# A row-wise log-sum-exp: late sums held in PSUM, an earlier word to SyncE, and a first load cut in three

## The chip, the cores and the metric

The kernel runs on one core of a Trainium2 chip. Its time is device time in microseconds (us), from launch to completion on that core. Three runs of the kernel before the change took 162.76, 163.02 and 163.10 us; the median is 163.02 us.

A core has five engines that matter here, each with an instruction queue of its own: TensorE (PE in the profile), VectorE (DVE), ScalarE (ACT), GpSimd (POOL) and SyncE (SP). They meet only through semaphores. Here SyncE issues every DMA transfer. A transfer is spread over 16 DMA engines, and its semaphore counts 16 when all of them are done.

## The reference

The input is 32 x 512 x 1024 float32 values, 67.1 MB. For each of the 16384 rows of 1024 values the result is one number:

```python
x_max = np.max(x, axis=axis, keepdims=True)
return (x_max.squeeze(axis) + np.log(np.sum(np.exp(x - x_max), axis=axis))).astype(np.float32)
```

Every input byte has to be read from memory once, an exponential has to be taken of every element, and 1024 of them have to be added for each row. The output is only 64 KB.

## The kernel before, in words

**Layout.** The 16384 rows are dealt over 128 partitions, 128 rows to a partition, so that partition p holds rows 128p to 128p+127. What the kernel calls a row (or a slot of its ring) is one such row in every partition: 128 x 1024 floats, 0.524 MB. 

**No maximum in the fast path.** The kernel takes `exp(x)` without subtracting the maximum, adds, and takes the logarithm. At the end it judges whether that was safe: all row sums must lie between `LOW` and `HIGH` (1e-18 and 1e18). Only if some sum does not, a branch (`nc.If`, line 278) does the whole work again with the maximum subtracted. With the input given here the branch's body is skipped.

**The stream.** The 128 rows are cut into 17 loads (`CHUNKS`, line 10) of 4, 15, 16, 16, 16, 14, 13, 9, 7, 5, 4, 3, 2 and four times 1 rows. Loads go into a ring of 51 rows (`ring`, line 74). `load(i)` (line 125) makes SyncE wait until the ring slots are free again and then issues the transfer; each load has its own semaphore `landed[i]`. ScalarE waits for it, takes exp in place (line 196, in one or two parts), and VectorE adds up the rows (line 216; some loads row by row with a fused add, line 203). A few rows are summed by ScalarE itself, through the accumulator that an activation can carry along (`accum_out`, lines 223 and 186). The loads are small at the end, so that little work is left when the last bytes land.

**What comes ahead of everything.** The instructions of the first load are moved by hand (lines 323 to 331) to the front of the program's head, ahead of the drain with which SyncE enters the barrier that all engines pass at the start. So the first transfer is issued at the very start of the profiled span, and the second only after the barrier.

**The late rows.** The last four rows (`LATE`) are loaded one by one and summed by ScalarE into four columns of `late`. In the kernel before, `late` is a part of an SBUF tensor `checked`, which has the columns LOW, late sums, HIGH side by side. 

**The end.** ScalarE takes the logarithm of the four late sums (line 152, called from line 234), and SyncE stores the result (line 237). Beside that runs the judgement: VectorE finds the largest and the smallest of the 124 earlier sums (lines 242 and 245) and puts them next to the late ones; when ScalarE has delivered the last sum, one comparison (line 252) tests `LOW < value` and `value < HIGH` together; TensorE adds the 128 x 12 answers over the partitions (line 257); VectorE adds them up to one number, `verdict` (line 262). SyncE, VectorE and ScalarE wait for it, load it into a register (line 267) and branch on it (line 278). Behind the branch VectorE and ScalarE each add one to the semaphore `passed` (lines 314 and 315). SyncE waits for two of these, clears the semaphores, waits for the store and is done (lines 316 to 319).

The diff touches one long function; it is printed here with the line numbers that the profile uses.

Of the kernel before, what the change touches and what calls it, by code (L numbers as in the profile page):

```python
# [17 lines left out]
RING_ROWS = 51  # L18


UNEVEN = ()
PARTS = ((0, 128, 2), (1, 128, 4), (3, 128, 8), (7, 64, 8), (71, 128, 8))


LN_AT = 7
# [6 lines left out]
LOW, HIGH = 1e-18, 1e18  # L32


STEPS = (43, 43, 42)
# [3 lines left out]
def kernel(  # L39
# [6 lines left out]
    nc = tc.nc  # L46
# [22 lines left out]
    spans = list(zip((0, *CUTS), (*CUTS, D)))  # L69
    assert 1 <= len(spans) <= 2  # L70
    n_late = LATE - 1 + len(spans)
    K = n_late + 2

    ring = nc.alloc_sbuf_tensor("ring", [P, RING_ROWS, D], fp32).ap()
    sums = nc.alloc_sbuf_tensor("sums", [P, NB], fp32).ap()
    res = nc.alloc_sbuf_tensor("res", [P, NB], fp32).ap()

    checked = nc.alloc_sbuf_tensor("checked", [P, 3 * K], fp32).ap()
    good = nc.alloc_sbuf_tensor("good", [P, 2 * K], bf16).ap()
    ones = nc.alloc_sbuf_tensor("ones", [P, 1], bf16).ap()  # L80
    verdict = nc.alloc_sbuf_tensor("verdict", [1, 1], int32).ap()
    peak = nc.alloc_sbuf_tensor("peak", [P, NB], fp32).ap()
    votes = nc.alloc_psum_tensor("votes", [P, 512], fp32).ap()
    late = checked[:, K : 2 * K]
    ALL_GOOD = P * 2 * K

    landed = [nc.alloc_semaphore(f"landed{i}") for i in range(len(CHUNKS) + len(spans) - 1)]
    act_done = nc.alloc_semaphore("act_done")
# [36 lines left out]
    def load(i):  # L125
        (s, row), r = place[i], CHUNKS[i][0]
        act_wait = max(a for a, _ in busy[s : s + r])
        dve_wait = max(d for _, d in busy[s : s + r])
        if dve_wait:
            nc.sync.wait_ge(dve_done, dve_wait)  # L130
        if act_wait:
            nc.sync.wait_ge(act_done, act_wait)
        dst, src = ring[:, s : s + r], x_v[:, row : row + r]
        if i == len(CHUNKS) - 1:
            for k, (lo, hi) in enumerate(spans):
                nc.sync.dma_start(out=dst[:, :, lo:hi], in_=src[:, :, lo:hi]).then_inc(
                    landed[i + k], 16
                )
        elif i in UNEVEN:
            for first, last, step in PARTS:  # L140
                nc.sync.dma_start(
                    out=dst[first:last:step], in_=src[first:last:step]
                ).then_inc(landed[i], 16)
        else:
            nc.sync.dma_start(out=dst, in_=src).then_inc(landed[i], 16)
# [20 lines left out]
    n_early = len(body.instructions)  # L166

    nc.scalar.preload_act_table_set("natural_log_exp_and_others")  # L168
    nc.gpsimd.memset(checked[:, :K], LOW)  # L169
    nc.gpsimd.memset(checked[:, 2 * K :], HIGH)  # L170
    nc.gpsimd.memset(ones, 1.0).then_inc(pool_done, 1)  # L171

    logged = 0
    done_before = [(0, 0)]
    for i, (r, n_dve, parts, by_halves) in enumerate(CHUNKS):
        if i:
            load(i)
        s, row = place[i]
        if i == LN_AT:
            logged = place[i - LN_LAG][1]  # L180
            take_logs(0, logged, sums[:, :logged], *done_before[i - LN_LAG])
        if i == len(CHUNKS) - 1:
            take_logs(logged, late_row, sums[:, logged:late_row], *done_before[-LATE])
            for k, (lo, hi) in enumerate(spans):
                nc.scalar.wait_ge(landed[i + k], 16)
                nc.scalar.activation(  # L186
                    out=ring[:, s, lo:hi],
                    in_=ring[:, s, lo:hi],
                    func=Exp,
                    accum_out=late[:, LATE - 1 + k : LATE + k],  # L190
                ).then_inc(act_done, 1)
                acts += 1
            continue
        nc.scalar.wait_ge(landed[i], 16 * (len(PARTS) if i in UNEVEN else 1))
        for lo, hi in cuts(n_dve, parts):
            nc.scalar.activation(  # L196
                out=ring[:, s + lo : s + hi], in_=ring[:, s + lo : s + hi], func=Exp
            ).then_inc(act_done, 1)
            acts += 1
            nc.vector.wait_ge(act_done, acts)  # L200
            if by_halves:
                for j in range(lo, hi):
                    nc.vector.tensor_tensor_reduce(  # L203
                        out=ring[:, s + j, : D // 2],
                        in0=ring[:, s + j, : D // 2],
                        in1=ring[:, s + j, D // 2 :],
                        scale=1.0,
                        scalar=0.0,
                        op0=Alu.add,
                        op1=Alu.add,  # L210
                        accum_out=sums[:, row + j : row + j + 1],
                    ).then_inc(dve_done, 1)
                    dves += 1
                    busy[s + j] = (0, dves)
            else:
                nc.vector.reduce_sum(  # L216
                    out=sums[:, row + lo : row + hi], in_=ring[:, s + lo : s + hi], axis=AX
                ).then_inc(dve_done, 1)
                dves += 1
                for j in range(lo, hi):  # L220
                    busy[s + j] = (0, dves)
        for j in range(n_dve, r):
            nc.scalar.activation(  # L223
                out=ring[:, s + j],
                in_=ring[:, s + j],
                func=Exp,
                accum_out=total(row + j),
            ).then_inc(act_done, 1)
            acts += 1
            busy[s + j] = (acts, 0)  # L230
        done_before.append((dves, acts))

    summed = acts
    take_logs(late_row, NB, late[:, : NB - late_row], dves, acts)

    nc.sync.wait_ge(act_done, acts)
    nc.sync.dma_start(out=out_v, in_=res).then_inc(stored, 16)


    nc.vector.wait_ge(act_done, done_before[-LATE][1])  # L240
    nc.vector.wait_ge(dve_done, dves)
    nc.vector.reduce_max(  # L242
        out=late[:, n_late : n_late + 1], in_=sums[:, :late_row], axis=AX
    ).then_inc(dve_done, 1)
    nc.vector.tensor_reduce(  # L245
        out=late[:, n_late + 1 : n_late + 2], in_=sums[:, :late_row], axis=AX, op=Alu.min
    ).then_inc(dve_done, 1)
    dves += 2
    nc.vector.wait_ge(pool_done, 1)
    nc.vector.wait_ge(dve_done, dves)  # L250
    nc.vector.wait_ge(act_done, summed)  # L251
    nc.vector.tensor_tensor(  # L252
        out=good, in0=checked[:, : 2 * K], in1=checked[:, K:], op=Alu.is_lt
    ).then_inc(dve_done, 1)
    dves += 1
    nc.tensor.wait_ge(dve_done, dves)
    nc.tensor.matmul(  # L257
        votes[:1, : 2 * K], lhsT=ones, rhs=good, start=True, stop=True
    ).then_inc(counted, 1)
    nc.vector.wait_ge(counted, 1)  # L260
    with nc.allow_low_precision(reason="whole numbers"):
        nc.vector.reduce_sum(out=verdict, in_=votes[:1, : 2 * K], axis=AX).then_inc(judged, 1)  # L262
# [7 lines left out]
    ends = [sum(STEPS[: k + 1]) for k in range(len(STEPS))]  # L270
    steps = [(end - n, end) for n, end in zip(STEPS, ends)]
    base_dve, base_act = dves, acts
    PIECES = 3

# [39 lines left out]
    nc.vector.sem_inc(passed, 1)  # L314
    nc.scalar.sem_inc(passed, 1)
    nc.sync.wait_ge(passed, 2)
    nc.sync.sem_clear(range(used[0], used[-1] + 1))
    nc.sync.wait_ge(stored, 16)
# [48 lines left out]
```

## Time and profile before

| | value |
|---|---|
| median of 3 runs | 163.02 us |
| the profiled execution, its own time | 163.09 us |
| its span, first to last instruction | 161.7 us |
| read from memory, mean rate over the span | 67.11 MB, 415 GB/s |
| time of the DMA packets, share of 16 engines' span | 96.9% |
| DVE busy | 121.8 us (75%), 50 instructions |
| ACT busy | 115.2 us (71%), 40 instructions |
| PE, POOL busy | 0.2 us, 0.4 us |

How to read it. The span is 1.4 us shorter than the execution's own time; what lies around it is the program's start and end. A group of instructions is given by its source line, engine and operation, with output <- input, shapes, count, then busy time and mean duration, and last the time that its engine sat idle ahead of it and what ended that wait. The chain that ended last is followed back from the last instruction: each piece is either work or a transfer that somebody waited for. Instructions that only wait, set a register, branch or add to a semaphore are not in the busy times, but waits on them are listed (as DVEq, SPq and so on, the engine's queue). The table of stretches gives, for each stretch of the span, its length, the busy time and the number of instructions of PE, its weight loads, DVE, ACT and POOL, then the granted clock of TensorE, the DMA share and the rate in GB/s. A packet is put down to the stretch where it began, so that short stretches can show shares over 1.

Behind these views the trace keeps a record of each DMA packet (begin, duration, size), of each semaphore step and of each instruction, waits and branches too. Where a number in this document comes from such a record, it says so.

### The profile page before, as it was taken

The page shows a single profiled execution, that of the slowest core. Times are in us where ns is not written, and L with a number is a line of the kernel's source. Part 1 is how long each engine was busy: PE and PEld are TensorE (multiplying, and loading weights), DVE is VectorE, ACT ScalarE, POOL GpSimd, SP SyncE. Part 2 cuts the span into 40 slices and gives each one's busy share as a digit, 9 for nine tenths or more (in the row PEclk, how much of TensorE's full clock was granted, in tenths as well). Part 3 has the DMA queues.
Part 4 walks back from the last instruction along what each step waited for, and adds up shares of the span by engine and source line. Part 5 has one row for each costly group of instructions (what it writes and reads, how often), then busy time and mean ns, then how long its engine had stood idle before and what let it go on. Part 6 is the DMA issues. An engine that isn't in the chain of part 4 may idle for free.

```text
span 161.7 us, 145 instructions
## 1 busy us (share of the span) xinstructions
PE 0.2 (0%) x1; PEld 0.1 (0%) x1; DVE 121.8 (75%) x50; ACT 115.2 (71%) x40; POOL 0.4 (0%) x7
## 2 busy tenths in 40 slices
PE   0000000000000000000000000000000000000000
PEld 0000000000000000000000000000000000000000
DVE  0028000004999999999999599999999999999793
ACT  3170006995089960999429993999199999999995
POOL 0000000000000000000000000000000000000000
DMA  7999699979979979979979999999999999999990
GB/s 259 503 486 471 274 471 519 470 308 519 470 308 519 470 308 519 470 308 519 470 318 411 454 454 438 421 421 421 457 429 429 404 440 416 412 442 406 412 373 16
DMA packets 2592, 67.18 MB, mean 415 GB/s; under 512 B 288, under 2 KB 416, under 8 KB 928
## 3 DMA queue, kind: packets, MB, share of 16 engines
q1 hardware_dynamic: 2592, 67.18, 96.9%
HBM read 67.11 MB, written 0.07 MB: 415 GB/s over the span
## 4 chain that ended last, share of the span: by engine, by line
DMA 49%; DVE 30%; ACT 20%; issue 0%; PE 0%; DVEq 0%
DMA ring<-in_x_dram 49%; DVE sums L216 29%; ACT ring L196 17%; ACT ring L223 2%; ACT ring L186 1%; ACT res L152 0%; PE votes L257 0%; DVE good L252 0%; DVE verdict L262 0%; DVEq L251 0%
## 5 line engine op out<-in xcount | busy, mean ns | idle before, releaser
L216 DVE TENSOR_REDUCE sums<-ring 128x8 f32<-128x8192 f32 (+5 forms) x14 | 111.2, 7994 | 37.1 <-ACT ring L196 37.1
L196 ACT ACTIVATE ring<-ring 128x8192 f32<-128x8192 f32 (+6 forms) x18 | 104.4, 5836 | 43.8 <-DMA ring<-in_x_dram 43.6
L203 DVE CUSTOM_DVE_ANT_0 ring<-ring 128x512 f32<-128x512 f32 x16 | 9.9, 688 | 0.0
L223 ACT ACTIVATE ring<-ring 128x1024 f32<-128x1024 f32 x8 | 8.3, 1041 | 0.0
L168 ACT ACT_TABLE_LOAD x1 | 1.3, 1283 | 0.8 <-PEq L348 0.8
L223 ACT ACTIVATION_READ_ACCUMULATOR ring<-ring 128x1 f32 x8 | 1.5, 187 | 0.0
L203 DVE DVE_READ_ACCUMULATOR2_ANT sums<- 128x1 f32 x16 | 1.3, 84 | 0.0
L186 ACT ACTIVATE ring<-ring 128x1024 f32<-128x1024 f32 x1 | 1.0, 1039 | 0.0
L252 DVE TENSOR_TENSOR good<-checked 128x12 bf16<-128x12 f32 x1 | 0.2, 170 | 1.0 <-ACT ring L186 1.0
L152 ACT ACTIVATE res<-sums 128x81 f32<-128x81 f32 (+1 forms) x2 | 0.5, 240 | 0.0
L242 DVE TENSOR_REDUCE checked<-sums 128x1 f32<-128x124 f32 x1 | 0.3, 282 | 0.1
L262 DVE TENSOR_REDUCE verdict<-votes 1x1 int32<-1x12 f32 x1 | 0.2, 158 | 0.3 <-PE votes L257 0.3
L257 PE MATMUL votes<-good,ones 128*1 128x12 bf16 x1 | 0.2, 172 | 159.9 <-DVE good L252 159.9
L245 DVE TENSOR_REDUCE checked<-sums 128x1 f32<-128x124 f32 x1 | 0.3, 271 | 0.0
L152 ACT ACTIVATE res<-checked 128x4 f32<-128x4 f32 x1 | 0.2, 205 | 0.0
L186 ACT ACTIVATION_READ_ACCUMULATOR ring<-ring 128x1 f32 x1 | 0.2, 186 | 0.0
L257 PEld LDWEIGHTS votes<-good,ones 128*1 128x1 bf16 x1 | 0.1, 79 | 159.9 <-DVE good L252 159.9
L169 POOL MEMSET checked<- 128x6 f32 x1 | 0.1, 105 | 0.3 <-POOLq L348 0.3
L170 POOL MEMSET checked<- 128x6 f32 x1 | 0.1, 104 | 0.0
L348 POOL MEMSET const-bfloat16-1.0<- 128x1 bf16 x1 | 0.1, 102 | 0.0
L348 POOL MEMSET const-uint8-127<- 128x1 uint8 x1 | 0.1, 102 | 0.0
L171 POOL MEMSET ones<- 128x1 bf16 x1 | 0.1, 102 | 0.0
(2 smaller groups left out, 0.2 us busy)
## 6 DMA issues: line engine op xcount, KB each, us to landing
ring<-in_x_dram SPq DMA_DIRECT2D x1, 7680.0 KB, 24.9
ring<-in_x_dram SPq DMA_DIRECT2D x1, 7168.0 KB, 28.7
ring<-in_x_dram SPq DMA_DIRECT2D x1, 6656.0 KB, 35.9
ring<-in_x_dram SPq DMA_DIRECT2D x1, 4608.0 KB, 20.2
ring<-in_x_dram SPq DMA_DIRECT2D x2, 2048.0 KB, 16.1
ring<-in_x_dram SPq DMA_DIRECT2D x1, 3584.0 KB, 28.3
ring<-in_x_dram SPq DMA_DIRECT2D x1, 2560.0 KB, 27.3
ring<-in_x_dram SPq DMA_DIRECT2D x4, 512.0 KB, 27.0
```

What stands on the lines that cost most here:

```text
L152: nc.scalar.activation(out=res[:, lo:hi], in_=src, func=Ln, bias=bias).then_inc(act_done, 1)
L168: nc.scalar.preload_act_table_set("natural_log_exp_and_others")
L186: nc.scalar.activation(out=ring[:, s, lo:hi], in_=ring[:, s, lo:hi], func=Exp, accum_out=late[:, LATE - 1 + k : LATE + k],).then_inc(act_d ...
L196: nc.scalar.activation(out=ring[:, s + lo : s + hi], in_=ring[:, s + lo : s + hi], func=Exp).then_inc(act_done, 1)
L203: nc.vector.tensor_tensor_reduce(out=ring[:, s + j, : D // 2], in0=ring[:, s + j, : D // 2], in1=ring[:, s + j, D // 2 :], scale=1.0, scal ...
L216: nc.vector.reduce_sum(out=sums[:, row + lo : row + hi], in_=ring[:, s + lo : s + hi], axis=AX).then_inc(dve_done, 1)
L223: nc.scalar.activation(out=ring[:, s + j], in_=ring[:, s + j], func=Exp, accum_out=total(row + j),).then_inc(act_done, 1)
L242: nc.vector.reduce_max(out=late[:, n_late : n_late + 1], in_=sums[:, :late_row], axis=AX).then_inc(dve_done, 1)
L245: nc.vector.tensor_reduce(out=late[:, n_late + 1 : n_late + 2], in_=sums[:, :late_row], axis=AX, op=Alu.min).then_inc(dve_done, 1)
L252: nc.vector.tensor_tensor(out=good, in0=checked[:, : 2 * K], in1=checked[:, K:], op=Alu.is_lt).then_inc(dve_done, 1)
L257: nc.tensor.matmul(votes[:1, : 2 * K], lhsT=ones, rhs=good, start=True, stop=True).then_inc(counted, 1)
L262: nc.vector.reduce_sum(out=verdict, in_=votes[:1, : 2 * K], axis=AX).then_inc(judged, 1)
```

## The change

It has four parts.

1. **The first load in three.** `SPLIT = (0,)` and `PARTS = ((0, 128, 4), (2, 128, 4), (1, 128, 2))`: load 0 is issued as three transfers, of partitions 0, 4, 8, ... (32 of them), of 2, 6, 10, ... (32), and of 1, 3, 5, ... (64). All three add to `landed[0]`, and ScalarE waits for 48. All three stand ahead of SyncE's barrier.
2. **Late sums in PSUM.** `late` becomes a PSUM tensor. ScalarE's accumulators are written there, and the last logarithm reads them there.
3. **The judgement in two comparisons.** `compare` tests values, broadcast over two columns, against LOW and HIGH with "greater". The two extremes of the early sums are compared ahead (0 to 2), the late sums when they are there (2 to K). Before the second, VectorE waits for `act_done >= acts`, which now includes the last logarithm; before, it waited for the last sum. TensorE uses two matmuls into one accumulation, with weights 1 for "above LOW" and -2048 for "above HIGH", and the good count is P*K.
4. **The word to SyncE ahead of the branch.** VectorE and ScalarE add to `passed` right after the load of the verdict. In the built program the addition is carried by that load itself; behind the branch only SyncE has instructions left.

GpSimd sets one more small constant. The order of the loads, exps and sums is unchanged.

```diff
-UNEVEN = ()
-PARTS = ((0, 128, 2), (1, 128, 4), (3, 128, 8), (7, 64, 8), (71, 128, 8))
+SPLIT = (0,)
+PARTS = ((0, 128, 4), (2, 128, 4), (1, 128, 2))
...
-    checked = nc.alloc_sbuf_tensor("checked", [P, 3 * K], fp32).ap()
-    good = nc.alloc_sbuf_tensor("good", [P, 2 * K], bf16).ap()
-    ones = nc.alloc_sbuf_tensor("ones", [P, 1], bf16).ap()
+    bounds = nc.alloc_sbuf_tensor("bounds", [P, 2, K], fp32).ap()
+    above = nc.alloc_sbuf_tensor("above", [P, 2, K], bf16).ap()
+    ends = nc.alloc_sbuf_tensor("ends", [P, 2], fp32).ap()
+    weights = nc.alloc_sbuf_tensor("weights", [P, 2], bf16).ap()
...
-    late = checked[:, K : 2 * K]
-    ALL_GOOD = P * 2 * K
+    late = nc.alloc_psum_tensor("late", [P, 512], fp32).ap()
+
+    ALL_GOOD = P * K
+    TOO_MANY = 2048.0
...
-        elif i in UNEVEN:
+        elif i in SPLIT:
             for first, last, step in PARTS:
                 nc.sync.dma_start(
                     out=dst[first:last:step], in_=src[first:last:step]
...
-        nc.scalar.wait_ge(landed[i], 16 * (len(PARTS) if i in UNEVEN else 1))
+        nc.scalar.wait_ge(landed[i], 16 * (len(PARTS) if i in SPLIT else 1))
...
-    summed = acts
     take_logs(late_row, NB, late[:, : NB - late_row], dves, acts)
...
+    def compare(lo, hi, values):
+        nonlocal dves
+        nc.vector.tensor_tensor(
+            out=above[:, :, lo:hi],
+            in0=values.unsqueeze(1).to_broadcast([P, 2, hi - lo]),
+            in1=bounds[:, :, lo:hi],
+            op=Alu.is_gt,
+        ).then_inc(dve_done, 1)
+        dves += 1
...
     nc.vector.wait_ge(pool_done, 1)
     nc.vector.wait_ge(dve_done, dves)
-    nc.vector.wait_ge(act_done, summed)
-    nc.vector.tensor_tensor(
-        out=good, in0=checked[:, : 2 * K], in1=checked[:, K:], op=Alu.is_lt
-    ).then_inc(dve_done, 1)
-    dves += 1
+    compare(0, 2, ends)
+    nc.vector.wait_ge(act_done, acts)
+    compare(2, K, late[:, :n_late])
     nc.tensor.wait_ge(dve_done, dves)
     nc.tensor.matmul(
-        votes[:1, : 2 * K], lhsT=ones, rhs=good, start=True, stop=True
+        votes[:1, :K], lhsT=weights[:, :1], rhs=above[:, 0], start=True, stop=False
+    )
+    nc.tensor.matmul(
+        votes[:1, :K], lhsT=weights[:, 1:], rhs=above[:, 1], start=False, stop=True
     ).then_inc(counted, 1)
...
     n_good = nc.values_load(verdict, engines=[eng.engine for eng in deciding])
+    nc.vector.sem_inc(passed, 1)
+    nc.scalar.sem_inc(passed, 1)
...
-    nc.vector.sem_inc(passed, 1)
-    nc.scalar.sem_inc(passed, 1)
     nc.sync.wait_ge(passed, 2)
```

More of the change, by code (lines that the diff above doesn't have):

```diff
@@ L71 @@
     n_late = LATE - 1 + len(spans)
-    K = n_late + 2
+    K = 2 + n_late
     ring = nc.alloc_sbuf_tensor("ring", [P, RING_ROWS, D], fp32).ap()
@@ L83 @@
     votes = nc.alloc_psum_tensor("votes", [P, 512], fp32).ap()
-    late = checked[:, K : 2 * K]
-    ALL_GOOD = P * 2 * K
+    late = nc.alloc_psum_tensor("late", [P, 512], fp32).ap()
+    ALL_GOOD = P * K
+    TOO_MANY = 2048.0
+    assert TOO_MANY > ALL_GOOD
     landed = [nc.alloc_semaphore(f"landed{i}") for i in range(len(CHUNKS) + len(spans) - 1)]
@@ L168 @@
     nc.scalar.preload_act_table_set("natural_log_exp_and_others")
-    nc.gpsimd.memset(checked[:, :K], LOW)
-    nc.gpsimd.memset(checked[:, 2 * K :], HIGH)
-    nc.gpsimd.memset(ones, 1.0).then_inc(pool_done, 1)
+    nc.gpsimd.memset(bounds[:, 0], LOW)
+    nc.gpsimd.memset(bounds[:, 1], HIGH)
+    nc.gpsimd.memset(weights[:, :1], 1.0)
+    nc.gpsimd.memset(weights[:, 1:], -TOO_MANY).then_inc(pool_done, 1)
     logged = 0
@@ L237 @@
     nc.sync.dma_start(out=out_v, in_=res).then_inc(stored, 16)
+    def compare(lo, hi, values):
[7 more added lines that the diff above has]
+        dves += 1
     nc.vector.wait_ge(act_done, done_before[-LATE][1])
     nc.vector.wait_ge(dve_done, dves)
-    nc.vector.reduce_max(
-        out=late[:, n_late : n_late + 1], in_=sums[:, :late_row], axis=AX
-    ).then_inc(dve_done, 1)
+    nc.vector.reduce_max(out=ends[:, :1], in_=sums[:, :late_row], axis=AX).then_inc(dve_done, 1)
     nc.vector.tensor_reduce(
-        out=late[:, n_late + 1 : n_late + 2], in_=sums[:, :late_row], axis=AX, op=Alu.min
+        out=ends[:, 1:], in_=sums[:, :late_row], axis=AX, op=Alu.min
     ).then_inc(dve_done, 1)
@@ L250 @@
     nc.vector.wait_ge(dve_done, dves)
-    nc.vector.wait_ge(act_done, summed)
-    nc.vector.tensor_tensor(
-        out=good, in0=checked[:, : 2 * K], in1=checked[:, K:], op=Alu.is_lt
-    ).then_inc(dve_done, 1)
-    dves += 1
+    compare(0, 2, ends)
+    nc.vector.wait_ge(act_done, acts)
+    compare(2, K, late[:, :n_late])
     nc.tensor.wait_ge(dve_done, dves)
     nc.tensor.matmul(
-        votes[:1, : 2 * K], lhsT=ones, rhs=good, start=True, stop=True
+        votes[:1, :K], lhsT=weights[:, :1], rhs=above[:, 0], start=True, stop=False
+    )
+    nc.tensor.matmul(
+        votes[:1, :K], lhsT=weights[:, 1:], rhs=above[:, 1], start=False, stop=True
     ).then_inc(counted, 1)
@@ L261 @@
     with nc.allow_low_precision(reason="whole numbers"):
-        nc.vector.reduce_sum(out=verdict, in_=votes[:1, : 2 * K], axis=AX).then_inc(judged, 1)
+        nc.vector.reduce_sum(out=verdict, in_=votes[:1, :K], axis=AX).then_inc(judged, 1)
     deciding = (nc.sync, nc.vector, nc.scalar)
@@ L267 @@
     n_good = nc.values_load(verdict, engines=[eng.engine for eng in deciding])
-    ends = [sum(STEPS[: k + 1]) for k in range(len(STEPS))]
-    steps = [(end - n, end) for n, end in zip(STEPS, ends)]
+    nc.vector.sem_inc(passed, 1)
+    nc.scalar.sem_inc(passed, 1)
+    steps = [(sum(STEPS[:k]), sum(STEPS[: k + 1])) for k in range(len(STEPS))]
     base_dve, base_act = dves, acts
```

## The prediction

> **What bounds the kernel now.** I read the chain that ended last first, because busy shares (DVE 75%, ACT 71%) do not say who holds the end.
>
> ```profile
> 31 pieces in order of time: start us, us, what
> 0.72 0.07 issue
> 0.78 24.93 DMA ring<-in_x_dram
> ...
> 122.33 24.68 DMA ring<-in_x_dram
> 147.01 0.02 issue
> 147.03 2.76 ACT ring L196
> 149.79 1.04 ACT ring L223 x2
> 150.84 4.46 ACT ring L196 x2
> 155.29 2.85 ACT ring L223 x5
> ...
> 158.54 1.05 ACT ring L186 x2
> 159.58 0.03 issue
> 159.61 0.05 DVEq L251
> 159.66 0.04 issue
> 159.70 0.18 DVE good L252
> ```
>
> The chain is a transfer that lands at 147.01 (load 10), and from there ScalarE without a pause to 159.58. Everything before is the stream of loads. Is the stream ever short of work? The table of stretches says no:
>
> ```profile
> core 0: us, PE busy (x) PEld busy (x) DVE busy (x) ACT busy (x) POOL busy (x), PEclk, DMA share, GB/s
> ...
> 25.00:64.00 39.00, 0.00 (x0) 0.00 (x0) 25.23 (x3) 26.95 (x3) 0.00 (x0) 1.00 1.00 432
> 64.00:100.00 36.00, 0.00 (x0) 0.00 (x0) 34.26 (x5) 28.08 (x6) 0.00 (x0) 1.00 0.99 428
> ...
> 150.00:157.00 7.00, 0.00 (x0) 0.00 (x0) 6.03 (x12) 7.00 (x7) 0.00 (x0) 1.00 1.01 413
> ```
>
> The 16 DMA engines are busy all the time, at 432 to 413 GB/s. So the stream is the bound: what moves its start by some amount moves every landing, and ScalarE's last stretch with it. The load ahead of that stretch (load 6) lands at 116.58 by the semaphore records, and ScalarE then runs to the end with 0.12 us idle, so it follows the landings. Then the start, in quarters of a microsecond:
>
> ```profile
> 0.75:1.00 0.25, 0.00 (x0) 0.00 (x0) 0.00 (x0) 0.22 (x1) 0.17 (x3) 1.00 0.00 0
> 1.00:1.25 0.25, 0.00 (x0) 0.00 (x0) 0.00 (x0) 0.25 (x1) 0.00 (x0) 1.00 1.34 262
> 1.25:1.50 0.25, 0.00 (x0) 0.00 (x0) 0.00 (x0) 0.25 (x1) 0.00 (x0) 1.00 0.82 197
> 1.50:1.75 0.25, 0.00 (x0) 0.00 (x0) 0.00 (x0) 0.25 (x1) 0.00 (x0) 1.00 1.27 393
> 1.75:2.00 0.25, 0.00 (x0) 0.00 (x0) 0.00 (x0) 0.25 (x1) 0.00 (x0) 1.00 0.71 197
> ```
>
> The first packets of the 16 engines begin at different times. The packet records give it: seven between 1.01 and 1.33 us, one at 1.57, eight between 1.64 and 1.88. The first packets end between 2.20 and 2.98 us; from then on each engine moves 16 KB in 0.611 us, one packet behind the other. This head start never closes. The 16 steps of `landed[0]` come at 6.85 to 7.58 us (13 of them by 7.22, then 7.36, 7.39, 7.58), those of load 1 at 25.00 to 25.71, those of load 6 at 115.80 to 116.58, those of the last load at 157.64 to 158.27. A load counts as landed only with its last engine, so about 0.3 to 0.5 us of every landing is the delay of the engines that began last.
>
> Last, the end. Who waits in SyncE's queue:
>
> ```profile
> SPq L237 <- ACT res L152: 29.2, 1, 29.2
> SPq L317 <- DVEq L314: 0.6, 1, 0.6
> ```
>
> The second line is the last wait of the kernel: SyncE waits 0.6 us at its clearing of the semaphores for VectorE's word behind the branch. By the instruction records all three engines branch at 160.93 to 160.96; ScalarE gives its word at 161.10, VectorE only at 161.53, SyncE clears at 161.57 and ends at 161.72. The store has landed at 161.38, so it does not hold the end; the judgement does.
>
> **Part 1, the first load.** The begins fit one descriptor stream, written in the order of partitions: two groups of eight engines, 0.6 us apart. [...] A list of 32 strided partitions passes all engines in a quarter of the time: (1.88 - 1.01) / 4 = 0.22 us, so all 16 begin by about 1.23. When they finish their first packet is less sure, since the early beginners took 1.38 us for it and one late beginner 0.61. I take the early ones as model: the seven ended at 2.20 to 2.54, so the last engine gains 2.98 - 2.54 = 0.44, less what random slow packets give back: 0.40. Bounds: a gain of 0.78 (last engine as early as the best, 2.98 - 2.20), and a loss, since no row here shows a load of fewer than 128 partitions: if the strided pieces made two engines share one way into SBUF, the 2.1 MB of load 0, 4.9 us at 429 GB/s (16 x 16 KB in 0.611), could take up to twice that, +4.9.
>
> Two more transfers in the queue cost something. The single-row loads at the end are queued in the same way: 413 against 432 GB/s is 1.27 against 1.21 us for 0.524 MB, 0.06 a transfer. With 16 KB packets kept I take 0.05 for both; bounds 0 and 0.12. [...]
>
> SyncE issues two more transfers ahead of the barrier: 2 x 0.35 (median of the issues) = 0.70 us later through it. Behind it wait the table load (0.78 to 2.06, then to 2.8; ScalarE needs it at 7.6), GpSimd's constants (0.95, then 1.7; needed at 159.7) and load 1's issue (0.78, then 1.5; its packets are due when load 0's run out, near 6.9). All are covered by load 0 itself; the cover ends only if they were 5 us late.
>
> **Parts 2 and 3, the judgement.** Before, the comparison began 0.12 after the last sum (159.58 to 159.70), through a separate wait. Now it waits for the logarithm, whose semaphore came at 159.82; a direct wait took 0.03 (TensorE's semaphore 160.11 to VectorE 160.14), so it begins at 159.85: +0.15. PSUM may shorten ScalarE's read of the accumulator (186 ns) and the logarithm (205 ns): bounds 0 and, if both dropped to the 170 ns of line 252, 0.05; I take 0.03. Behind that wait on VectorE stands only the verdict; TensorE waits for it, then all three deciding engines. The comparison stays at 170 ns (the PSUM read of line 262 took 158). The early comparison falls into VectorE's 1.0 us of idle time before line 252. The second matmul: bounds 0 and a whole one with its weights, 0.17; I take a weight load, 0.06 to 0.08. Sum: 0.15 - 0.03 + 0.07 = +0.19; bounds +0.10 and +0.32.
>
> The store starts no later, up to 0.05 earlier, and is not the end.
>
> **Part 4, the word.** VectorE's word now rides on its verdict load, which ended at 160.92 before. SyncE is then held by its own branch alone. How long that takes the trace doesn't show, as SyncE was waiting: ScalarE went on 0.16 after its branch began, VectorE 0.57. From SyncE's 160.93 that is 161.10 or 161.50 against 161.57: a saving of 0.07 to 0.47. SyncE skips 13 instructions, VectorE 11, ScalarE 6, so the slow row is nearer. But VectorE's late return may still count for the time behind the span (163.09 - 161.72 = 1.37), if the program's end waits for all engines. I take 0.24. With the judgement's +0.19 the end moves by -0.05; bounds -0.37 and +0.25.
>
> **Sum.** -0.40 + 0.05 - 0.05 = -0.40 on 163.09 in the profiled execution; that execution lies 0.07 over the median, so 162.6 against 163.02.
>
> **Rivals.**
> - *The last engine stays last.* For it: first packets that began 0.6 us apart ended almost together, so something else than the list may gate them. Then the start gives nothing and the end -0.05 to +0.1: 163.0.
> - *The strided pieces collide (slower).* Place: load 0, 1.0 to 7.6 us. If half of its 4.9 us ran at two thirds of the rate, it costs 2.45 x 0.5 = 1.2, with nothing gained: 164.2; full collision 167.9. It decides from 0.7 us on (more than the 0.40 gained plus the 0.33 that can be told), that is, when 14% of the load's time is lost. For it: no such row. Against it: all 16 engines have the same number of bytes, and packets stay 16 KB.
> - *The word does nothing and the judgement is longer.* SyncE's own branch is as slow as VectorE's, TensorE pays both matmuls in full, and the start gives nothing: 163.02 + 0.25 to 0.35, 163.3.
>
> **How the numbers follow.** Forecast 52% (own range 162.3 to 162.85), last engine stays last 20%, collision 20%, longer judgement 8%. About 0.2% (0.33 us) is what a measurement can tell from no change, so faster means below 162.69: 40 of the forecast's 52. Same: its other 12 and 18 of the second case, 30. Slower: 20 + 8 + 2 = 30. The range goes from 162.2 (both parts near their better bounds) to 164.0, which leaves out the larger collisions and a little below, under 2 in 10.
>
> **What would show it.** Right: begins of the 16 first packets within 0.3 us, landing of load 0 near 7.15 instead of 7.58, load 10 near 146.6 instead of 147.01; comparison 0.1 to 0.2 after ScalarE's logarithm began; no wait of SyncE for VectorE at its last clear. Wrong: a landing of load 0 later than 7.6, or an early landing whose gain is gone by load 6, or a SyncE that clears later than 161.57 less the gain of the stream.

## The result, and the profile after

The changed kernel takes 163.60 us, the median of seven runs (163.42 to 164.12). The kernel before, run beside it, takes 162.76 us (162.71 to 163.10, seven runs). The ratio of the runs is 1.0045, with a 95% interval of 1.0032 to 1.0059. The change makes the kernel slower, by 0.84 us between the medians; 0.4 us faster was predicted. The profiled execution took 163.42 us, with a span of 161.70 us.

The stretches of the start, in the same columns as those of before:

```profile
core 0: us, PE busy (x) PEld busy (x) DVE busy (x) ACT busy (x) POOL busy (x), PEclk, DMA share, GB/s
...
1.00:1.25 0.25, 0.00 (x0) 0.00 (x0) 0.00 (x0) 0.00 (x0) 0.00 (x0) 1.00 0.00 0
1.25:1.50 0.25, 0.00 (x0) 0.00 (x0) 0.00 (x0) 0.00 (x0) 0.00 (x0) 1.00 1.34 393
1.50:1.75 0.25, 0.00 (x0) 0.00 (x0) 0.00 (x0) 0.00 (x0) 0.00 (x0) 1.00 1.00 262
1.75:2.00 0.25, 0.00 (x0) 0.00 (x0) 0.00 (x0) 0.00 (x0) 0.00 (x0) 1.00 1.20 328
2.00:5.00 3.00, 0.00 (x0) 0.00 (x0) 0.00 (x0) 1.28 (x1) 0.20 (x4) 1.00 0.95 333
...
25.00:64.00 39.00, 0.00 (x0) 0.00 (x0) 24.62 (x2) 26.95 (x3) 0.00 (x0) 1.00 1.00 435
64.00:100.00 36.00, 0.00 (x0) 0.00 (x0) 34.44 (x5) 28.09 (x6) 0.00 (x0) 1.00 1.00 434
```

The stretch from 2 to 5 us before the change (in both kernels only packets of load 0 begin in it):

```profile
2.00:5.00 3.00, 0.00 (x0) 0.00 (x0) 0.00 (x0) 0.06 (x1) 0.00 (x0) 1.00 0.97 415
```

Three things are to be seen. In 1.00 to 1.25 us no packet begins; before, four did. In 2 to 5 us the DMA engines are about as busy as before (0.95 against 0.97), but begin packets worth only 333 GB/s; the same stretch of before has 415. And from 25 us on the rate is no lower than it was (435 and 434 GB/s, before 432 and 428), so the loss is made in the first load and carried on. The packet records say the same: the 16 first packets begin at 1.33 to 2.04 us (before: 1.01 to 1.88), and an engine spends 5.72 us on its share of load 0's packets (before: 5.33).

The chain that ended last:

```profile
31 pieces in order of time: start us, us, what
2.40 0.06 issue
2.46 23.86 DMA ring<-in_x_dram
...
122.76 24.72 DMA ring<-in_x_dram
147.48 0.02 issue
147.50 2.76 ACT ring L201
150.26 1.04 ACT ring L228 x2
151.30 4.45 ACT ring L201 x2
155.75 3.01 ACT ring L228 x6
...
158.80 1.11 ACT ring L191 x2
159.91 0.02 issue
159.93 0.18 ACT res L156
160.11 0.02 issue
160.13 0.18 DVE above L246
160.31 0.04 issue
160.36 0.17 PE votes L267
160.52 0.04 PE votes L270
160.56 0.02 issue
160.59 0.15 DVE verdict L275
```

Load 1 is issued at 2.46 us instead of 0.78, lands at 26.32 instead of 25.71, and load 10 at 147.48 instead of 147.01. From there ScalarE runs on as before. The chain now goes through the last logarithm (line 156) ahead of the comparison, and through a second matmul (line 270), which by the instruction records ends 0.03 us after the first. By the landing records load 0 is complete at 8.16 us (before 7.58), load 6 at 117.06 (116.58), the last load at 158.73 (158.27).

Who waits in SyncE's queue at the end:

```profile
SPq L331 <- SPq L331: 0.2, 1, 0.2
SPq L329 <- DVEq L280: 0.2, 1, 0.2
```

The wait of 0.6 us for VectorE's word behind the branch is gone. What is left, 0.2 us each, is a wait at the clearing of the semaphores for the word that VectorE's verdict load carries, and one for the store. The groups of the new end (busy us, mean ns, idle time ahead):

```profile
L156 ACT ACTIVATE res<-late 128x4 f32<-128x4 f32 x1 | 0.2, 173 | 0.0
L191 ACT ACTIVATION_READ_ACCUMULATOR ring<-ring 128x1 f32 x1 | 0.2, 152 | 0.0
L246 DVE TENSOR_TENSOR above<-late,bounds 128x8 bf16<-128x8 f32 x1 | 0.2, 168 | 0.7 <-ACT res L156 0.7
L275 DVE TENSOR_REDUCE verdict<-votes 1x1 int32<-1x6 f32 x1 | 0.2, 151 | 0.3 <-PE votes L270 0.3
```

The same two instructions of ScalarE before:

```profile
L152 ACT ACTIVATE res<-checked 128x4 f32<-128x4 f32 x1 | 0.2, 205 | 0.0
L186 ACT ACTIVATION_READ_ACCUMULATOR ring<-ring 128x1 f32 x1 | 0.2, 186 | 0.0
```

With the late sums in PSUM the read of the accumulator takes 152 ns instead of 186, and the last logarithm 173 instead of 205.

**How the time comes apart.** In the twelve profiles with the end of before, the execution's time is the landing of the last load plus 4.82 to 4.88 us. In the four with parts 2 to 4 it is that landing plus 4.69 to 4.71, and with one half of them alone plus 4.74 and 4.75. So every kernel here comes apart into a stream, which ends with a landing, and an end. For the profiled pair: 158.73 - 158.27 = +0.46 by the stream, -0.13 by the end, +0.33 together (163.42 against 163.09). The medians differ by more than this pair, since these two executions lie at the lower end of the runs of after and the upper end of those of before.

### The profile page after: what moved, and what is told of

It reads as the page before. It is cut to its first block, busy times and chain, and to the rows that moved or that the text cites. A ratio compares the mean times of both kernels' runs of the same rounds, so it can differ in the third digit from the quotient of the medians.

```text
span 161.7 us, 149 instructions
## 1 busy us (share of the span) xinstructions
PE 0.2 (0%) x2; PEld 0.1 (0%) x2; DVE 121.9 (75%) x51; ACT 115.1 (71%) x40; POOL 0.4 (0%) x8
## 4 chain that ended last, share of the span: by engine, by line
DMA 48%; DVE 30%; ACT 20%; issue 0%; PE 0%
DMA ring<-in_x_dram 48%; DVE sums L221 29%; ACT ring L201 17%; ACT ring L228 3%; ACT ring L191 1%; ACT res L156 0%; DVE above L246 0%; PE votes L267 0%; DVE verdict L275 0%; PE votes L270 0%
## 5 line engine op out<-in xcount | busy, mean ns | idle before, releaser
L256 DVE TENSOR_REDUCE ends<-sums 128x1 f32<-128x124 f32 x1 | 0.3, 282 | 0.1
L257 DVE TENSOR_REDUCE ends<-sums 128x1 f32<-128x124 f32 x1 | 0.3, 271 | 0.0
```

What stands on the lines that cost most here:

```text
L256: nc.vector.reduce_max(out=ends[:, :1], in_=sums[:, :late_row], axis=AX).then_inc(dve_done, 1)
L257: nc.vector.tensor_reduce(out=ends[:, 1:], in_=sums[:, :late_row], axis=AX, op=Alu.min).then_inc(dve_done, 1)
```

## The experiments

The theory formed from the two traces was: the strided cut of load 0 costs time, because its pieces start later and their packets take longer; everything else in the change is about neutral. The rivals were: the late issue of load 1 leaves the queue short; any cut into three costs a fixed time per transfer; the new judgement or the word takes the time. In each comparison below, the time of before is that of the same chip.

### Each part alone

**Part 1 alone**, in the kernel before:

```diff
-UNEVEN = ()
-PARTS = ((0, 128, 2), (1, 128, 4), (3, 128, 8), (7, 64, 8), (71, 128, 8))
+UNEVEN = (0,)
+PARTS = ((0, 128, 4), (2, 128, 4), (1, 128, 2))
```

> The kernel before with part 1 alone: load 0 as three strided transfers, all ahead of the barrier; judgement and branch as before. Theory A (the start is the loss): the three issues hold SyncE 0.55 to 0.6 us each as in the profile of the changed kernel, load 0's packets begin at about 1.3 instead of 1.0 us and some take 1.0 us instead of 0.61, load 1 lands near 26.3 instead of 25.7, and the run is 0.4 to 0.7 us slower than before. Theory B (the end is the loss: judgement and branch): the run is within 0.2 us of before. The theory on record (the last engine gains 0.40): 0.3 us faster; the profile of the changed kernel already speaks against it.

Measured: 163.76 against 162.78 us, ratio 1.0060 [1.0039, 1.0081]. Part 1 alone costs all of the loss. Its profiled execution (164.53 us, the slowest of its six) shows where, in the timeline of the start (begin us, us, instruction, idle time ahead and what ended it):

```profile
0.00 1.81 SPq L141 DMA_DIRECT2D ring<-in_x_dram  x3
2.46 1.28 ACT L168 ACT_TABLE_LOAD   x1 [2.46 <-PEq L348]
...
9.16 3.62 ACT L196 ACTIVATE ring<-ring 128x4096 f32<-128x4096 f32 x1 [5.41 <-DMA ring<-in_x_dram]
...
27.32 13.00 ACT L196 ACTIVATE ring<-ring 128x15360 f32<-128x15360 f32 x1 [14.54 <-DMA ring<-in_x_dram]
```

The three issues take 1.81 us, ScalarE's first exp begins at 9.16 and the second at 27.32; in the kernel before these were 7.61 and 25.73:

```profile
7.61 3.62 ACT L196 ACTIVATE ring<-ring 128x4096 f32<-128x4096 f32 x1 [5.54 <-DMA ring<-in_x_dram]
...
25.73 13.00 ACT L196 ACTIVATE ring<-ring 128x15360 f32<-128x15360 f32 x1 [14.51 <-DMA ring<-in_x_dram]
```

This execution holds one more thing: a single packet of load 0 that took 2.07 us, so that one engine was 1.16 us behind the mean of all at load 1.

**Parts 2 to 4 without part 1**, in the changed kernel:

```diff
-SPLIT = (0,)
+SPLIT = ()
```

> The changed kernel with load 0 in one transfer again: parts 2, 3 and 4 alone. Theory A: within 0.25 us of before (comparison 0.11 later, VectorE's return from the branch about 0.1 later), SyncE no longer waits 0.6 us at its clear. Theory B: 0.5 to 0.8 us slower than before, as slow as the changed kernel.

Measured: 162.69 against 162.78 us, 0.9990 [0.9980, 1.0000]. The timeline is back where it was:

```profile
7.41 3.62 ACT L201 ACTIVATE ring<-ring 128x4096 f32<-128x4096 f32 x1 [5.35 <-DMA ring<-in_x_dram]
...
25.52 13.00 ACT L201 ACTIVATE ring<-ring 128x15360 f32<-128x15360 f32 x1 [14.50 <-DMA ring<-in_x_dram]
```

1.0060 x 0.9990 is 1.0050, against 1.0045 for the whole change: the parts add up.

**Part 4 alone**, the word ahead of the branch, in the kernel before:

```diff
     n_good = nc.values_load(verdict, engines=[eng.engine for eng in deciding])
+    nc.vector.sem_inc(passed, 1)
+    nc.scalar.sem_inc(passed, 1)
...
-    nc.vector.sem_inc(passed, 1)
-    nc.scalar.sem_inc(passed, 1)
     nc.sync.wait_ge(passed, 2)
```

> The kernel before with part 4 alone: VectorE and ScalarE give their word with the load of the verdict, ahead of the branch. If the end of the program waits for SyncE's clear alone, the time falls by as much as the span, 0.1 to 0.45 us. If it waits for every engine, VectorE's return from the branch (0.57 us after the branch began) holds it, and the time falls by 0.15 us at most while the span falls more.

Measured: 162.84 against 162.78 us, 1.0000 [0.9988, 1.0012]. SyncE's wait is gone from its queue as in the whole change:

```profile
SPq L317 <- DVEq L267: 0.2, 1, 0.2
```

**Parts 2 and 3 alone**: as parts 2 to 4, with the word back behind the branch.

```diff
-SPLIT = (0,)
+SPLIT = ()
...
     n_good = nc.values_load(verdict, engines=[eng.engine for eng in deciding])
-    nc.vector.sem_inc(passed, 1)
-    nc.scalar.sem_inc(passed, 1)
...
+    nc.vector.sem_inc(passed, 1)
+    nc.scalar.sem_inc(passed, 1)
     nc.sync.wait_ge(passed, 2)
```

> The kernel before with parts 2 and 3 alone: late sums in PSUM and the judgement in two comparisons; load 0 in one transfer, the word behind the branch. The step on record was +0.19 (bounds +0.10 and +0.32). From the profiles, the branch of VectorE begins 0.08 later after the last activation than before. So 0.05 to 0.2 us slower than before, and SyncE waits about 0.6 us for VectorE's word again.

Measured: 162.92 against 162.94 us, 1.0000 [0.9985, 1.0015]. The wait is there again, a little longer:

```profile
SPq L329 <- DVEq L326: 0.7, 1, 0.7
```

So neither half of the end can be told from nothing by its times. The instruction records are finer. The first two rows below add up to the time from the last landing to the end of the execution; the third is a part of the second (us):

| piece of the end | before | word alone | judgement alone | both, no cut | after |
|---|---|---|---|---|---|
| last landing to VectorE's branch | 2.68 | 2.72 | 2.61 | 2.67 | 2.66 |
| VectorE's branch to the end of the execution | 2.14 | 2.03 | 2.14 | 2.02 | 2.03 |
| end of the span to the end of the execution | 1.37 | 1.61 | 1.37 | 1.71 | 1.72 |

The second row takes only two values: 2.13 to 2.15, over all profiles, where VectorE still has a word to give behind its branch, 2.02 to 2.03 where it has not (2.05 in the shortened retry below). The third row moves instead: SyncE is done earlier, the span ends earlier, and the time behind the span grows. Counted from ScalarE's branch, the time to the end varies more, from 2.06 to 2.22 us. So the execution's end follows VectorE's return from the branch and not SyncE's last instruction. The word saves 0.11 us of a possible 0.46 (the time from SyncE's branch to its clearing falls from 0.64 to 0.18).

**A shorter retry.** If VectorE's return depends on how much code it skips, less code behind the branch should shorten it. This kernel leaves out steps two and three of the three steps of the retry, which the given input doesn't use.

```diff
+    steps = steps[:1]
     base_dve, base_act = dves, acts
```

> The changed kernel with load 0 in one transfer, and with the body of the branch cut to its first step: it leaves out steps two and three of the retry, so a retry would do only 43 of 128 rows. The body is skipped with this input. VectorE then skips 5 instructions where it skipped 11, ScalarE 3 or 4, SyncE 7. If the time that an engine needs to come back from the branch grows with what it skips, VectorE's return falls from 0.57 us towards ScalarE's 0.16, and the run is 0.2 to 0.4 us faster than the run without the split (which was 0.1% under before), 162.3 to 162.5 where before is 162.8. If VectorE is slow at any branch, no change.

Measured: 162.82 against 162.94 us, 0.9993 [0.9980, 1.0006], and 2.05 us from VectorE's branch to the end. That is no gain on 2.02 to 2.03. That idea falls; what VectorE's return waits for stays open.

### Is it the late issue of load 1?

**Load 1 issued late, load 0 whole.** SyncE waits ahead of load 1 until GpSimd has written 44 more columns of a scratch tensor.

```diff
+    for k in range(44):
+        nc.gpsimd.memset(peak[:, k : k + 1], 0.0)
     nc.gpsimd.memset(ones, 1.0).then_inc(pool_done, 1)
...
+        if i == 1:
+            nc.sync.wait_ge(pool_done, 1)
         if i:
             load(i)
```

> The kernel before with load 0 in one transfer, and with load 1's issue held back to about 2.5 us (SyncE waits for GpSimd, which sets 44 more single columns first); nothing else changes. In the changed kernel load 1 was issued at 2.47 instead of 0.78. If the late issue of load 1 is the cause of the loss, this run is 0.4 to 0.9 us slower than before and load 1 lands at 26 or later. If the cause is in load 0's own packets, it is within 0.2 us of before, since load 0's packets run until 7 us.

Measured: load 1 is issued at 2.43 us, nearly as late as in the changed kernel, and the time is 163.32 against 163.20 us, 0.9998 [0.9986, 1.0010]. The late issue costs nothing.

**Loads 1 to 3 issued ahead of the barrier too**, with load 0 whole and parts 2 to 4:

```diff
-SPLIT = (0,)
+SPLIT = ()
...
-    load(0)
+    for i in range(4):
+        load(i)
...
-        if i:
+        if i > 3:
             load(i)
```

> The changed kernel with load 0 in one transfer (as in the run without the split), and with loads 1, 2 and 3 also issued ahead of the barrier, since none of them waits for a ring slot. If early lists help the engines, 0.1 to 0.3 us faster than the run without the split, 162.4 to 162.6. If the loads behind load 0 never run short, the same as that run, 162.7; the barrier then comes at about 2.5 us and costs nothing.

Measured: 163.06 against 163.20 us, 0.9993 [0.9984, 1.0002], the same as without it (0.9990). Early issue gains nothing, and the barrier, passed at 2.45 us instead of 0.72, costs nothing.

### Which property of the cut costs?

**A cut by rows.** Three transfers of 1, 1 and 2 rows, each on all 128 partitions, in the kernel before:

```diff
-UNEVEN = ()
-PARTS = ((0, 128, 2), (1, 128, 4), (3, 128, 8), (7, 64, 8), (71, 128, 8))
+UNEVEN = (0,)
+PARTS = ((0, 1), (1, 2), (2, 4))
...
-            for first, last, step in PARTS:
+            for lo, hi in PARTS:
                 nc.sync.dma_start(
-                    out=dst[first:last:step], in_=src[first:last:step]
+                    out=dst[:, lo:hi], in_=src[:, lo:hi]
```

> The kernel before with load 0 in three transfers, all ahead of the barrier, but cut by rows: 1, 1 and 2 rows of all 128 partitions in place of 32, 32 and 64 partitions with 4 rows. The same bytes and the same number of transfers. If the stride or the small number of partitions is what costs (theory A1), each issue takes about 0.37 us, the first packets begin within 0.3 us of each other and no later than 1.05, and the run is within 0.2 us of before or up to 0.3 faster. If the number of transfers ahead of the barrier is what costs (theory A2), the run is 0.3 to 0.7 us slower, like the strided one.

Measured: 163.28 against 162.78 us, 1.0038 [1.0020, 1.0057]. The start is what the prediction had hoped for from part 1: the issues take 0.38 to 0.43 us, all 16 engines begin between 1.00 and 1.31 us, and the stretches show packets from 1.00 on.

```profile
1.00:1.25 0.25, 0.00 (x0) 0.00 (x0) 0.00 (x0) 0.00 (x0) 0.00 (x0) 1.00 0.74 180
1.25:1.50 0.25, 0.00 (x0) 0.00 (x0) 0.00 (x0) 0.00 (x0) 0.00 (x0) 1.00 1.19 279
```

And yet nothing is gained: load 1 lands in the mean over its engines at 25.19 us (before 25.28), its last engine at 25.77 (before 25.71). Two more executions of it follow, one run each.

> A second profile of the row cut. If the last engine's lag is what varies, the last load's mean landing stays near 157.66 (as in its first profile) and a slower execution shows a lag over the 0.52 seen there, up to 1.5 us. If the whole stream varies, the lag stays near 0.5 and the mean moves. In both cases the execution's time is the last landing of the last load plus 4.84, as in all profiles of kernels with the old judgement.

> A third profile of the row cut. Lag varies: mean of the last load near 157.66, lag over 0.52 in a slower execution. Stream varies: lag near 0.5, mean moves. Time is the last landing plus 4.84 either way.

Measured: 163.67 and 163.41 us, beside 162.92 of before. The mean landing of load 1 is 25.65 and 25.23, the last engine 0.75 and 0.51 us behind it. The last load lands at 158.18, 158.83 and 158.57 in the three profiles. The seven kernels with load 0 whole have 157.94 to 158.43, 158.23 in the mean. Both the mean and the last engine's delay vary here. Against those seven, the last load's mean landing is 0.06 us later on average and its last engine lags 0.60 us behind the mean instead of 0.37; three profiles can't settle the shares.

**The same cut as part 1, twice more**, to see whether its long packet comes always.

> A second profile of the strided cut alone. The mean landing of the last load stays 0.5 to 0.7 over the 157.9 of one transfer (158.4 to 158.6) if the late begin and the long packets of load 0 set it; the lag of the last engine, 1.11 in the first profile, falls to 0.3 to 0.6 if that was one chance packet of 2.07 us.

> A third profile of the strided cut alone: mean landing of the last load 158.4 to 158.6 if load 0's late begin and long packets set it; lag of the last engine 0.3 to 0.6 if the 1.11 of the first profile was chance.

Measured: 164.67 and 163.66 us, beside 162.92, one run each. The mean landing of the last load is 158.40 and 158.45, as expected of the late begin and the long packets. The first has again one packet of 2.06 us in load 0, and its last engine is 1.45 us behind the mean at load 1; the second has none over 1.25 us and a last engine 0.34 us behind. Two of the four profiles with this cut have such a packet. In the seven kernels with load 0 whole the longest packet of load 0 takes 1.31 to 1.63 us.

**Pieces of the same size without a stride.** This edit and the three after it start from the kernel with part 1 alone:

```diff
-PARTS = ((0, 128, 4), (2, 128, 4), (1, 128, 2))
+PARTS = ((0, 32, 1), (32, 64, 1), (64, 128, 1))
```

> The kernel before with load 0 cut by partitions as in the changed kernel (32, 32 and 64, all ahead of the barrier), but into contiguous ranges 0-31, 32-63, 64-127 instead of strided ones. If the stride makes the issue long (theory A1a), each issue takes about 0.38 to 0.43 us as in the row cut and the first packet begins at 1.0. If the small number of partitions does (A1b), the issues take 0.55 to 0.6 and the first packet begins at 1.3. If packets of two engines slow each other when they go to neighbouring partitions, more of load 0's packets take over 0.7 us than with the stride and load 0 lands later than 8.2.

Measured: 167.51 against 163.20 us, 1.0257 [1.0241, 1.0272]. Here is a loss of the size that the prediction gave to the full collision, 4.3 us where it had 4.9. The stretch from 2 to 8 us runs at about half of load 0's full rate of 429 GB/s (16 x 16 KB in 0.611 us):

```profile
2.00:5.00 3.00, 0.00 (x0) 0.00 (x0) 0.00 (x0) 1.28 (x1) 0.17 (x3) 1.00 1.14 246
5.00:8.00 3.00, 0.00 (x0) 0.00 (x0) 0.00 (x0) 0.00 (x0) 0.00 (x0) 1.00 0.91 197
```

126 of load 0's 128 packets take over 1.0 us; the median is 1.27, where the kernel before has 0.61. An engine spends 9.85 us on load 0. No run shows why the packets take twice as long. Two things are nevertheless as in the kernel before: the first issue takes 0.39 us, and the first packet begins at 1.02 us. So a first piece of 32 partitions doesn't start late because it is small (1.02 us in one block); it starts late because it is strided (1.33 us in part 1).

**Two strided halves, and four strided quarters:**

```diff
-PARTS = ((0, 128, 4), (2, 128, 4), (1, 128, 2))
+PARTS = ((0, 128, 2), (1, 128, 2))
```

```diff
-PARTS = ((0, 128, 4), (2, 128, 4), (1, 128, 2))
+PARTS = ((0, 128, 4), (2, 128, 4), (1, 128, 4), (3, 128, 4))
```

> The kernel before with load 0 in two strided transfers, partitions 0, 2, 4, ... and 1, 3, 5, ... (64 each), both ahead of the barrier. If each strided transfer costs for itself (issue 0.55 to 0.6, slow first packets), the loss lies between before and the three-way cut: 0.3 to 0.7 us; load 1 lands at 25.9 to 26.3. If only the very small pieces of 32 cost, it is within 0.2 us of before.

> The kernel before with load 0 in four strided transfers of 32 partitions each (0, 4, 8, ...; 2, 6, ...; 1, 5, ...; 3, 7, ...), all ahead of the barrier. If pieces of 32 slow their own packets (two engines sharing), a DMA engine spends more on load 0 than in the three-way cut: 6.1 to 6.8 us where that cut has 5.8 to 5.9 and one transfer 5.4, and the run is 0.9 to 1.6 us slower than before. If only the first transfers after the start are slow, it is like the three-way cut, 0.6 to 1.0 us slower.

Measured: the halves take 163.41 against 163.20 us, 1.0011 [1.0001, 1.0021]; the quarters 163.92 against 162.94, 1.0065 [1.0040, 1.0090]. Both begin at 1.33 us, and their first issues take 0.55 us, as in part 1.

**The same three pieces, the one of 64 first:**

```diff
-PARTS = ((0, 128, 4), (2, 128, 4), (1, 128, 2))
+PARTS = ((1, 128, 2), (0, 128, 4), (2, 128, 4))
```

> The kernel before with the three strided transfers of the changed kernel in another order: the 64 partitions first, then 32 and 32. If pieces of 32 slow their own packets wherever they stand, a DMA engine again spends 5.8 to 6.0 us on load 0 and the run is 0.5 to 1.0 us slower. If it is the cold start of the pieces that costs, 5.4 to 5.6 us, and 0.1 to 0.4 us slower, as with two halves.

Measured: 163.29 against 162.94 us, 1.0025 [1.0010, 1.0040], by the ratios less than half of what the same pieces cost in the order of the change (1.0060 [1.0039, 1.0081]). The timeline shows the same late start, and a first exp on time:

```profile
0.00 1.82 SPq L141 DMA_DIRECT2D ring<-in_x_dram  x3
...
7.63 3.62 ACT L196 ACTIVATE ring<-ring 128x4096 f32<-128x4096 f32 x1 [3.88 <-DMA ring<-in_x_dram]
```

In the stretch from 2 to 5 us it is back at 404 GB/s, where the order of the change has 333:

```profile
2.00:5.00 3.00, 0.00 (x0) 0.00 (x0) 0.00 (x0) 1.28 (x1) 0.17 (x3) 1.00 0.97 404
```

So these pieces of 32 strided partitions are not slow wherever they stand; they are slow when they stand first: an engine spends 5.28 us on load 0 with the 64 first, 5.76 in the mean with part 1's order.

By the times alone, a fixed cost for each transfer isn't ruled out: leaving aside the pieces without stride, two cost 0.11%, three cost 0.25, 0.38 and 0.60%, four cost 0.65%. Against it as the whole cause stand the order of the same three pieces, and the records that follow.

### The start, accounted for

All from the packet and landing records of the profiled executions, in us; lines of several profiles give the mean, and the range where it matters. "Packets" is the time that an engine spends on load 0's packets, which are told from load 1's by their size. (An expectation above puts it at 5.8 to 5.9 for part 1 and 5.4 for one transfer; told by size, the first two profiles of part 1 have 5.72 and 5.91, that of the kernel before 5.33.) "Worked out" is the later mean begin plus the longer packets, against the first line; "measured" is the shift of load 1's mean landing.

| load 0 as | first begins | mean begin | packets | worked out | measured | last engine behind the mean at load 1 |
|---|---|---|---|---|---|---|
| one transfer (7 profiles) | 1.00 to 1.02 | 1.36 | 5.40 | | (25.27; 25.15 to 25.40) | 0.26 to 0.64 |
| part 1 (4 profiles) | 1.33 to 1.34 | 1.62 | 5.76 | +0.62 | +0.69 | 0.34 to 1.45 |
| strided quarters | 1.33 | 1.65 | 5.55 | +0.44 | +0.69 | 0.38 |
| strided halves | 1.33 | 1.61 | 5.39 | +0.24 | +0.42 | 0.32 |
| the 64 first | 1.35 | 1.66 | 5.28 | +0.18 | +0.17 | 0.39 |
| rows (3 profiles) | 1.00 to 1.01 | 1.23 | 5.47 | -0.06 | +0.09 | 0.51 to 0.75 |
| without stride | 1.02 | 1.17 | 9.85 | +4.26 | +4.75 | 0.36 |

The seven profiles of one transfer differ by 0.25 us among themselves, so that shifts of 0.09 and 0.17 in the last rows can't be told from nothing. In part 1 the two terms give nearly the whole shift: 0.26 because strided pieces begin late, 0.36 because packets take longer. What is left can be found too: the halves' 0.18 in load 1's own packets (18.38 us an engine instead of 18.20), the quarters' 0.25 in gaps between packets (0.26 us an engine instead of 0.01). On top comes, in some executions of part 1, the one packet of about 2 us. At the last load the four profiles of part 1 have a mean landing 0.57 us later than the seven, and a last engine 0.82 us behind the mean instead of 0.37. Together that is 1.02 us, close to the 0.98 us that part 1 costs, and not quite half of it is the last engine.

## Why the prediction was wrong

**The step that failed: "so all 16 begin by about 1.23 ... the last engine gains ... 0.40".** It failed in three ways.

- *The begin.* That a list of 32 partitions passes all engines in a quarter of the time, 0.22 us, was the author's estimate; no run shows it. The time to the first packet the step left as it was. Measured, a strided transfer holds SyncE for 0.55 us instead of 0.38, and its first packet begins 0.33 us later. The spread of the begins didn't shrink either: 1.33 to 2.04 is 0.71 us (before 0.87).
- *The packets.* They stayed at 16 KB, as the prediction had it. But the step took the early first packets of before as model for the first ones, and counted nothing for the later ones beyond some random slow packets. In the changed kernel not only the first packet of each engine is slow: 38 of load 0's 128 packets take over 0.70 us; in the kernel before 16 do. Some come at 4.1 to 4.8 us, well after the start.
- *What a cut keeps.* With load 0 whole, no engine leaves more than 0.06 us between two packets of loads 0 and 1 by the packet records, so that each can be followed. There the head start is handed on, as the prediction had it: in the kernel before, the engine whose first packet ends last, 0.46 us behind the mean, is also the last at load 1, 0.43 behind, and over the 16 engines the two times go together (correlation 0.97; in five other kernels with load 0 whole 0.62 to 0.98). But cut pieces bring new differences. The three profiles of the row cut have begins only 0.31 to 0.51 us apart (before 0.87), and the last engine ends its first 16 KB 0.16, 0.35 and 0.33 us behind the mean; it ends load 0 0.60, 0.91 and 0.54 behind, through longer later packets and gaps. At load 1 the lag is then 0.51 to 0.75 us. In part 1 it is 0.34 to 1.45. So no cut tried here got the 0.40, not even the one with the early, narrow begins.

The prediction's own sign of being wrong, "a landing of load 0 later than 7.6", came at 8.16 us. That 163.60 us lies between the ends of the stated range, 162.2 and 164.0, owes nothing to this step, which had the wrong direction.

**Two more transfers, +0.05 (0 to 0.12).** No run isolates it. What the two terms of the table leave over is 0.18 us with two transfers, 0.07 and -0.01 with three strided ones, 0.15 with three by rows and 0.25 with four: nothing that grows steadily with the number of transfers, and at most 0.18 for an added one. All of part 1, with its two transfers more, costs 0.98 us.

**The issues, 0.35 each.** Mis-sized: they take 0.55, 0.57 and 0.59 us, and the drain behind them 0.37 instead of 0.13, so that SyncE passes the barrier at 2.40 us, 1.68 later and not 0.70. That load 0 covers all that waits behind it was right, as the late load 1 showed (0.9998).

**Judgement, +0.19 (0.10 to 0.32).** The terms were there, but the sum had the wrong sign. From the end of the last sum to the begin of the verdict it is 0.69 us instead of 0.56: +0.13, with the second matmul at 0.03 instead of 0.07. Against it stand two gains that the prediction had put at 0.03 or not seen. From the last landing to the end of the last sum it is 1.17 instead of 1.30 us: ScalarE's reads are some 0.03 us shorter each with PSUM (the last 152 ns instead of 186), so that its last exp begins 0.07 us behind the landing instead of 0.17. (The log of 43 early sums just ahead isn't shorter, 0.24 against 0.22.) And the load of the verdict takes 0.54 instead of 0.59 us on VectorE. Alone, the judgement comes 0.08 us earlier to VectorE's branch.

**Word, -0.24 (0.07 to 0.47).** SyncE goes on 0.18 us after its branch begins, about as soon as ScalarE, not as late as VectorE, so "the slow row is nearer" was wrong. The gain is nevertheless 0.11 only, by the risk that the prediction named: the end of the execution waits for VectorE's return, and comes 2.03 us after VectorE's branch with the word alone, 2.14 before. The word riding on the load also makes VectorE later to branch by 0.04 us (2.72 us after the last landing instead of 2.68). "The store ... is not the end" did not hold for the span: SyncE's last instruction begins at 161.69 us, right after the store has landed at 161.67. It held for the execution, whose end follows VectorE.

**The end as a whole, -0.05 (-0.37 to +0.25).** Measured -0.13 in the profiles, and 0.9990 [0.9980, 1.0000] without part 1. This lies inside the bounds, but by luck: from the landing to the end the judgement alone gives 4.74 us instead of 4.82 where +0.19 was forecast, and the word alone 4.75 where -0.24 was; the two errors cancel.

**The rivals.** "The strided pieces collide" came nearest: its place was right (load 0), its sign too, and the price of part 1, 0.98 us, lies near its 1.2, in part by chance, as nearly half of it is the last engine. But no run shows its mechanism, two engines that share one way. Long packets over the whole load are what the pieces without stride show, 1.27 us in the median instead of 0.61, at 4.3 us; the strided ones begin late, at 1.33 to 1.35 us instead of 1.00 to 1.02, and lose more in their packets only in the orders that put the pieces of 32 first. "The last engine stays last" was right as far as it went; it missed the losses. The longer judgement did not come.

**What stays open.** Why the packets of the pieces without stride take twice as long. Why the pieces of 32 are slow only when they stand first. Where the packets of some 2 us come from. Why the row cut, with its early begins, has longer later packets and gaps, and loses 0.4%. How much of the losses is a fixed cost for each transfer. And what VectorE waits for behind its branch.

**A better version.** None clearly beats the kernel before. Parts 2 to 4 without the cut are the best, at 0.9990 [0.9980, 1.0000].

## What to carry to other kernels

When a stream bounds a kernel, the form of its first transfer has to be measured, up to the landings: here the cuts by stride began late (mean begin 1.61 to 1.66 us instead of 1.36), the cut by rows began early (1.23), and all lost against one transfer over all 128 partitions, 0.11 to 0.65% and 0.38%. The row cut brought the begins from 0.87 us apart to 0.31 to 0.51, and its last engine was still 0.51 to 0.75 us behind the mean at load 1: whether the packets behind keep what the begins gain is seen by following the engines one by one. And where a last wait is taken away from one engine, ask which other engine the end of the execution waits for: here the word alone took 0.11 us from the time between VectorE's branch and the end of the execution, and the time behind the span grew from 1.37 to 1.61 us.

## What was not expected of the hardware

- The strided partition lists lengthened the first issue on SyncE from 0.38 or 0.39 us to 0.55, and delayed the first packet from 1.02 to 1.33 us, with 32 partitions or 64. A first piece of 32 partitions in one block did neither (0.39 and 1.02 us).
- After the branch on the verdict SyncE goes on in 0.18 us (after) and ScalarE in 0.16 (before); VectorE takes 0.57 (before). The input makes all three skip the body. A body of one third of the steps did not shorten the end (2.05 us from VectorE's branch, 2.02 with the whole body).
- With its target in PSUM instead of SBUF, ScalarE's last read of an accumulator took 152 ns (after) instead of 186 (before), and the logarithm of four columns from there 173 instead of 205.
- In the kernel before no engine leaves more than 0.06 us between two packets of loads 0 and 1, and 0.46 us of delay at the end of one engine's first packet are still 0.43 us at the end of load 1, 23 us later.
- Load 0 took packets of 2.06 and 2.07 us in two of four profiles with the cut of part 1, and that one engine's delay lasted to the last landing: 1.10 and 1.39 us behind the mean there.
